# Second feed-forward matrix in seven block products

## The chip, the cores and the metric

One core of one Trainium2 chip runs the whole program. The metric is the device time of one execution in microseconds (us). The kernel before takes 877.99 us, the median of three runs (877.97 to 878.5).

## The reference

One decoder layer over 512 tokens of 1024 channels, float32. A combined projection feeds three token mixers (sparse attention, a gated recurrence, a short convolution), whose gated sum is projected and added to `x`. The part that changes is the last line:

```python
h = _rmsnorm(x, ln_mlp_g[l])
x = x + jnp.square(jax.nn.relu(h @ w_mlp_up[l])) @ w_mlp_down[l]
```

`w_mlp_up` is 1024 x 4096, `w_mlp_down` 4096 x 1024. The norm divides by the root of the mean square `ms + eps`; since relu squared is homogeneous of degree 2, the kernel leaves the division out of the first product and divides the second by `ms + eps`.

## The kernel before

Activations lie channel by token: a tile is 128 channels by 512 tokens. Weights come in slabs of 128 x 1024 float32 (512 KB each, `slabs_of` and `_layout`), loaded by SP's queue into three `raw` tiles (`loader`). `splitter` makes two reduced-precision tiles of each: `whi`, a copy rounded by ScalarE (L296), and `wlo`, what is left, subtracted by VectorE (L300). Every product of float32 values is then three TensorE matmuls (L334) into one PSUM bank: high by high, high by low, low by high, each with a 128 x 128 stationary block and up to 512 moving columns.

The order of work is written once, when the kernel is built. `make_plan` lists the weight tiles; the main task issues their matmuls in that order, and all other work is a set of tasks that a planner (`Order`) places by costs and ready times into each engine's instruction order. Each engine then runs its list in order; between engines semaphores hold what isn't ready. `Get` takes a buffer from a numbered pool (tags such as `whi`, `wlo` with four tiles, `w2` with 55, `w4` with six), `Need` waits for a named result, `spawn` starts a task (priority 0 or 1), and work of priority 1 is not placed over 0.9 us ahead of TensorE's planned time (`LIM`).

In the feed-forward part the plan has two halves: 16 up tiles (128 inner channels each, eight contraction steps, 24 matmuls of 512 columns), then eight down tiles over those 16 inner tiles (48 matmuls of 512 columns, `tall`). `ev_up` takes an up tile out of PSUM: relu and square on ScalarE, square again and the low part on VectorE. `ev_dn` multiplies a down tile by the reciprocal of the mean square (`R2`); in the first half GpSimd adds it to the residual tile `X1`, in the second VectorE adds and SP's queue stores the result.

Of the kernel before, what the change touches and what calls it, by code (L numbers as in the profile page):

```python
# [16 lines left out]
ALU = mybir.AluOpType  # L17
# [30 lines left out]
def slabs_of(name, j):  # L48

    if name in FIRST_COL:  # L50
        return [("in", 0, 8, FIRST_COL[name] + 128 * j, 128)]
    if name == "kv":
        return [("kv", 0, 3, 0, 324), ("kv", 384, 3, 0, 324), ("kv", 768, 2, 0, 324)]
    if name in ("hi", "aq"):
        return [("in", 256 * i, 2, C_HI if name == "hi" else C_AQ, 512) for i in range(4)]
    if name[0] == "u" and name != "up":
        return [(name, 0, 4, 512 * j + 256 * i, 256) for i in range(2)]
    if name in ("wo", "up"):
        return [(name, 0, 8, 128 * j, 128)]
    return [("dn", 2048 * (j // 8) + 1024 * i, 8, 128 * (j % 8), 128) for i in range(2)]  # L60


SLABS = [p for name, j in PLAN for p in slabs_of(name, j)]


class Op:
    __slots__ = ("e", "c", "ins", "outs", "f")

    def __init__(self, e, c, ins, outs, f):
        self.e, self.c, self.f = e, c, f  # L70
# [24 lines left out]
class Order:  # L95
# [41 lines left out]
    def run(self, op):  # L137
        start = max([self.clk[op.e], self.clk["PE"]] + [self.seen(k, op.e) for k in op.ins])
        end = start + op.c
        self.clk[op.e] = end  # L140
        if op.e == "D":
            end += 2000
# [107 lines left out]
def kernel(ctx: ExitStack, tc: tile.TileContext, xT, x, first_d, slabs, vecs, rel, ident_d, masks_d,  # L250
# [9 lines left out]
    def maker(pool, tag, shape, n):  # L260
# [4 lines left out]

    tags = {t: maker(pool, t, s, n) for t, pool, s, n in (
        ("raw", sp, (128, 1024), 3), ("whi", sp, (128, 1024), 4), ("wlo", sp, (128, 1024), 4),
        ("w2", sp, (128, 512), 55), ("w4", sp, (128, 1024), 6), ("am", sp, (128, 512), 2),
        ("p", sp, (128, 1280), 2), ("cmb", sp, (128, 1280), 1), ("st", sp, (128, 16), 8),
        ("toep", sp, (128, 2048), 1), ("acc", pp, (128, 512), 4), ("aux", pp, (128, 512), 4))}  # L270
    o = Order(tags)
# [56 lines left out]
    def mm(ps, a, b, start, stop):  # L328
        n = size(b)
        if a.dtype == F32R:  # L330
            c = 0.4167 * n + 13.5 if n >= 192 else 213
        else:
            c = 2 * max(0.84 * n, 55 if size(a) <= 64 else 0.65 * size(a)) + 4
        return Op("PE", c, [a, b] + ([] if start else [ps]), [ps], lambda: PE.matmul(ps, a, b, start=start, stop=stop))  # L334

    def tr(ps, a):
        k = a.shape[0]
# [56 lines left out]
    def loader():  # L394
        for k in range(8):
            r = yield Get("w4", "raw0")
            yield dma(r[:, :896], first_d[:, 896 * k:896 * (k + 1)], nbytes=896 * 512)
            put(("raw0", k), r)
        for n in range(NSL):
            r = yield Get("raw", "raw")  # L400
            w = SLABS[n][2] * SLABS[n][4]
            yield dma(r[:, :w], slabs[n][:, :w], nbytes=1 << 19)
            put(("raw", n), r)
            if n < 2:
                for tb in ((0, 1), (2, 3))[n]:
                    for i in range(2):
                        t = yield Get("w2", "xt")
                        yield dma(t, x[:, tb, 512 * i:512 * (i + 1)], nbytes=1 << 18)
                        put(("xt", tb, i), t)
            if n == 1:  # L410
                yield dma(ident, ident_d, nbytes=1 << 16)
                yield dma(caus, caus_d, nbytes=1 << 16)
            if n == 4:
                yield dma(masks.rearrange("p a b -> p (a b)"), masks_d, nbytes=1 << 18)

    def first():
        for k in range(8):
# [15 lines left out]
            put(("xl", k), xl[k])  # L433
            free(r)

    def splitter():
        for n in range(NSL):
            r = yield Need(("raw", n))
# [315 lines left out]
    def soft_task():  # L754
# [5 lines left out]
        for h in range(8):  # L760
# [14 lines left out]
            for tb in range(4):  # L775
# [9 lines left out]
        for t in mbs[1:]:  # L785
            free(t)

    def soft_block(h, tb, pl, pb, cb, st, p):
        n = pb.shape[1]
# [199 lines left out]
    def ev_wo(m, ps):  # L989
# [17 lines left out]
        if m == 7:  # L1007
            pm = yield Get("aux", "pm")
            yield mm(pm, ones, ssum[0], True, True)
            free(ssum[0])  # L1010
            yield ts(R2, pm, EPS, None, ALU.add)
            free(pm)
            yield recip(R2, R2)
            put("R2", True)

    def ev_up(m, ps):
        rl = yield Get("w2", "rl")
        yield act(rl, ps, AF.Relu)
        free(ps)
        hi_t = yield Get("w2", "hh", F32R)  # L1020
        yield act(hi_t, rl, AF.Square)
        yield tt(rl, rl, rl, ALU.mult)
        lo_t = yield Get("w2", "hl", F32R)
        yield tt(lo_t, rl, hi_t.bitcast(F32), ALU.subtract)
        free(rl)
        put(("h", m), (hi_t, lo_t))

    def ev_dn(f, m, ps):
        yield Need("R2")
        if f == 0:  # L1030
            t = yield Get("w2", "t")
            yield tt(t, ps, R2, ALU.mult)
            free(ps)
            yield tt(X1[m], X1[m], t, ALU.add, "G")
            free(t)
            put(("x1", m), True)
            return
        yield Need(("x1", m))
        t = yield Get("w2", "o")
        parts = 2 if m == 7 else 1  # L1040
        w = 512 // parts
        for i in range(parts):
            q = slice(w * i, w * (i + 1))
            yield tt(t[:, q], ps[:, q], R2[:, q], ALU.mult)
            yield tt(t[:, q], t[:, q], X1[m][:, q], ALU.add)
            yield o.ready[key(t)]
            yield dma(out[128 * m:128 * (m + 1), q], t[:, q], [t], nbytes=(1 << 18) // parts)
        free(ps, t)


    def cols(n, m0, name, ev, rhs):
# [87 lines left out]
            spawn(ev_iq(i, ps[i]), 0)  # L1139
        spawn(EV["hf"](0, ps[2]), 0)  # L1140

    def tall(n, f, m):
        ps = yield Get("acc", "Adn")
        for i in range(2):
            h, l, h3, l3 = yield Need(("w", n + i))
            for k in range(8):
                bh, bl = yield Need(("h", 16 * f + 8 * i + k))
                yield [mm(ps, h3[:, k], bh, i + k == 0, False), mm(ps, h3[:, k], bl, False, False),
                       mm(ps, l3[:, k], bh, False, i == 1 and k == 7)]
            free(h, l)  # L1150
        spawn(ev_dn(f, m, ps), 0)
# [4 lines left out]
    def main():  # L1156
        yield from start()
        n = 0
        for name, j in PLAN:
# [24 lines left out]
            elif name == "kv":  # L1184
                yield from rows(n, cnt, name, ev_kv, xc, 324)
            elif name in ("aq", "hi"):
                yield from rows(n, cnt, name, ev_rows(name), ncl, 512)
            elif name == "wo":
                yield from cols(n, j, name, ev_wo, mr)
                if j == 7:  # L1190
                    for k in range(8):
                        free(*S["mx", k])
            else:
                yield from tall(n, j // 8, j % 8)
                if j % 8 == 7:
                    for k in range(16):
                        free(*S["h", 16 * (j // 8) + k])
            n += cnt

    o.ready[key(vec)] = 1500.0  # L1200
# [39 lines left out]

def _layout(inp):
    w = {"in": inp["w_in"][0], "u0": inp["w_up_attn"][0], "u1": inp["w_up_hgrn"][0], "u2": inp["w_up_conv"][0],
         "wo": inp["w_out"][0], "up": inp["w_mlp_up"][0], "dn": inp["w_mlp_down"][0]}
# [40 lines left out]
```

## Time and profile before

| | |
|---|---|
| median of three runs | 877.99 us |
| profiled execution | 877.3 us |
| its span, first to last instruction | 875.5 us |
| matmuls and weight loads on TensorE | 4140 each |
| VectorE, ScalarE, GpSimd instructions | 953, 593, 67 |
| HBM read, written | 87.15 MB, 3.68 MB |

PE is TensorE, PEld its loads of the stationary block, DVE VectorE, ACT ScalarE, POOL GpSimd, SP the queue that issues most DMAs. A matmul's duration in a row runs from its start to the end of its results, so that neighbours overlap; the spacing of starts is what a matmul costs in a stream. In a group of instructions "out<-in" names tiles, and "idle before" is the time in which the engine stood before them, with what ended it. A wait row names who waited for whom.

### The profile page before, as it was taken

The numbers are of one execution on the slowest core, as the hardware profiler recorded it, in microseconds if no ns is written. First come the engines' busy times: TensorE is split into PE (matmuls) and PEld (weight loads), VectorE is DVE, ScalarE is ACT, GpSimd is POOL, SyncE is SP. The second block draws the span as 40 slices with busy tenths as digits, with TensorE's granted clock in tenths as the row PEclk, the third lists the DMA queues.
The fourth block names the chain that finished last, engine by engine and source line by source line (L and its number), as shares of the span: only waits on it lengthen the run. The fifth ranks groups of instructions, "written<-read, shape, count | busy, mean of one in ns | idle before, by whom it ended". The sixth has DMA issues, their size and how long they took to land.

```text
span 875.5 us, 10712 instructions
## 1 busy us (share of the span) xinstructions
PE 870.0 (99%) x4140; PEld 725.8 (83%) x4140; DVE 522.9 (60%) x953; ACT 357.6 (41%) x593; POOL 67.8 (8%) x67
## 2 busy tenths in 40 slices
PE   9999999999999999999999999999999999999997
PEld 7988888888888888888888888888888888888886
DVE  5679888888877785668438545444433344443331
ACT  7773435235443465656533443333111133331110
POOL 0001000020000211225000230000111100000000
PEclk9999999999999999999999999999999999999999
DMA  9553222222222212222224322222223222223310
GB/s 347 210 197 143 96 89 80 73 86 83 72 73 73 95 51 73 72 73 74 96 73 157 133 99 92 97 97 97 96 97 97 97 96 97 97 97 124 122 67 24
DMA packets 28587, 89.95 MB, mean 103 GB/s; under 512 B 3152, under 2 KB 5880, under 8 KB 28536
## 3 DMA queue, kind: packets, MB, share of 16 engines
q1 hardware_dynamic: 28392, 89.25, 29.6%
q8 instruction: 32, 0.52, 0.2%
q14 instruction: 19, 0.16, 0.1%
q10 hardware_dynamic: 144, 0.02, 0.0%
HBM read 87.15 MB, written 3.68 MB: 104 GB/s over the span
## 4 chain that ended last, share of the span: by engine, by line
PE 99%; DVE 0%; issue 0%
PE Aup L334 20%; PE Adn L334 20%; PE Ag L334 15%; PE Au L334 8%; PE Awo L334 5%; PE Acb L334 3%; PE Ahg L334 3%; PE Ach L334 3%; PE Aaq L334 3%; PE Acc L334 3%; PE Ahq L334 2%; PE Ahi L334 2%; PE pa L334 2%; PE Ahf L334 2%; PE Akv L334 2%; PE Ast L334 2%
## 5 line engine op out<-in xcount | busy, mean ns | idle before, releaser
L300 DVE TENSOR_TENSOR wlo<-raw,whi 128x1024 fp32r<-128x1024 f32 (+2 forms) x150 | 188.6, 1258 | 91.9 <-ACT whi L296 86.5
L296 ACT ACTIVATE whi<-raw 128x1024 fp32r<-128x1024 f32 (+2 forms) x150 | 153.9, 1026 | 217.8 <-PE Adn L334 120.1
L334 PE MATMUL Aup<-x2h,whi 128*128 128x512 f32 x256 | 100.0, 391 | 0.0
L334 PE MATMUL Aup<-x2h,wlo 128*128 128x512 f32 x256 | 99.6, 389 | 0.0
L334 PE MATMUL Aup<-x2l,whi 128*128 128x512 f32 x256 | 99.6, 389 | 0.0
L334 PE MATMUL Adn<-hh,whi 128*128 128x512 f32 x256 | 99.6, 389 | 0.0
L334 PE MATMUL Adn<-hl,whi 128*128 128x512 f32 x256 | 99.6, 389 | 0.0
L334 PE MATMUL Adn<-hh,wlo 128*128 128x512 f32 x256 | 99.6, 389 | 0.0
L334 PE MATMUL Ag<-nh,whi 128*128 128x512 f32 x192 | 78.1, 407 | 0.0
L300 DVE TENSOR_TENSOR rl<-rl 128x512 f32<-128x512 f32 x32 | 22.1, 692 | 91.4 <-ACT hh L296 91.4
L334 PE MATMUL Ag<-nh,wlo 128*128 128x512 f32 x192 | 75.2, 392 | 0.0
L334 PE MATMUL Ag<-nl,whi 128*128 128x512 f32 x192 | 75.0, 390 | 0.0
L296 ACT ACTIVATE rl<-Aup 128x512 f32<-128x512 f32 x32 | 19.1, 598 | 110.2 <-PE Aup L334 110.2
L334 PE MATMUL Au<-yp,whi 128*128 128x512 f32 x192 | 60.9, 398 | 0.0
L334 PEld LDWEIGHTS Aup<-x2l,whi 128*128 128x128 f32 x256 | 48.0, 188 | 10.3 <-issue 0.2
L334 PEld LDWEIGHTS Aup<-x2h,whi 128*128 128x128 f32 x256 | 48.0, 188 | 10.2 <-issue 0.2
L334 PEld LDWEIGHTS Adn<-hh,whi 128*128 128x128 f32 x256 | 48.0, 188 | 10.0
L334 PEld LDWEIGHTS Adn<-hl,whi 128*128 128x128 f32 x256 | 48.0, 188 | 10.0
L334 PEld LDWEIGHTS Aup<-x2h,wlo 128*128 128x128 f32 x256 | 48.1, 188 | 9.9
L334 PEld LDWEIGHTS Adn<-hh,wlo 128*128 128x128 f32 x256 | 48.0, 188 | 9.9
L334 PEld LDWEIGHTS Ag<-nh,wlo 128*128 128x128 f32 x192 | 36.0, 188 | 8.1
L334 PEld LDWEIGHTS Ag<-nh,whi 128*128 128x128 f32 x192 | 36.1, 188 | 6.2
(257 smaller groups left out, 1609.1 us busy)
## 6 DMA issues: line engine op xcount, KB each, us to landing
raw<-in_slabs_dram SPq DMA_DIRECT2D x139, 512.0 KB, 3.2
raw<-in_first_dram SPq DMA_DIRECT2D x8, 448.0 KB, 5.4
xt<-in_x_dram SPq DMA_DIRECT2D x8, 256.0 KB, 6.6
xr<-in_xT_dram SPq DMA_DIRECT2D x8, 256.0 KB, 4.0
x<-in_xT_dram SPq DMA_DIRECT2D x4, 512.0 KB, 5.9
out_dram<-o SPq DMA_DIRECT2D x7, 256.0 KB, 2.0
d<-d SPq DMA_DIRECT2D x1, 1536.0 KB
toep<-d SPq DMA_DIRECT2D x1, 1024.0 KB, 6.6
```

What stands on the lines that cost most here:

```text
L296: return Op("A", c, [in_, scale, bias], [out_, accum], lambda: A.activation(out_, in_, func, **kw))
L300: return Op(e, c, [a, b], [out_], lambda: (V if e == "V" else G).tensor_tensor(out_, a, b, op))
L334: return Op("PE", c, [a, b] + ([] if start else [ps]), [ps], lambda: PE.matmul(ps, a, b, start=start, stop=stop))
```

## The change

The second matrix is multiplied by 2 x 2 x 2 blocks with seven products in place of eight (Winograd's variant of Strassen's form). The 4096 inner channels are taken in four parts; each part holds four pairs of up tiles, and its down products follow when the part is ready: the plan has 9, 8, 8 and 7 up tiles ahead of the four parts. A unit is one part and one pair of output tiles, so there are 16. In it A is 2 x 2: output tile by half of the pair, 128 x 512 of weights each; B is 2 x 2: half of the pair by half of the tokens, 256 columns each.

- Weights (`seven`, `halves`): S1 = a21 + a22 is made by a plain load of a22 and an accumulating DMA of a21 from GpSimd's queue; S2 = S1 - a11, S3 = a11 - a21, S4 = a12 - S2 on VectorE; then a11|a12 and S2|S3 (1024 columns), S1, S4 and a22 (512) are split in high and low parts. The low part of a22 is made by a second accumulating DMA onto the negated high part.
- Activations (`ev_up`, `pair_of`): of each pair T1 = b12 - b11, T2 = b22 - T1, T3 = b22 - b12, T4 = b21 - T2 on VectorE, all split in high and low parts.
- Products (`twin_units`): two units take turns, step by step, one in the `acc` and one in the `aux` banks. Step 0 is a11 b11, step 1 a12 b21, then S2 T2, S3 T3, S1 T1, a22 T4, S4 b22. Step 2 and later ones add onto a bank that an earlier step left; before that the bank's content has been added to `X1`, and the step waits for it (`wait`).
- `ev_dn` adds each step's bank (256 columns) to `X1` on VectorE: seven for a unit. `X1` is multiplied by the mean square ahead of it, on GpSimd, and by the reciprocal at the end, on VectorE.
- The planner's cost of a matmul under 320 columns is 3 ns less; `Op` has a latency `lat`; `w2` has one tile more.

```diff
-    for f in range(2):
-        plan += [("up", 16 * f + j) for j in range(16)] + [("dn", 8 * f + j) for j in range(8)]
+    ups = [("up", j) for j in range(32)]
+    for c, (i, j) in enumerate(((0, 9), (9, 17), (17, 25), (25, 32))):
+        plan += ups[i:j] + [("dn", 4 * c + m) for m in range(4)]
...
+    def add_dma(out_, in_, ins):
+        return Op("G", 900, ins + [out_], [out_], lambda: G.dma_start(out_, in_, accum_op=ALU.add), 4600)
...
+            if n in UNITS:
+                g = yield Get("w4", "s1")
+                yield dma(g[:, :512], slabs[n + 1][:, 512:], nbytes=1 << 18)
+                yield add_dma(g[:, :512], slabs[n + 1][:, :512], [])
+                put(("s1", n), g)
...
+    def halves(src, w, name, big=True, dma_=False):
+        h = yield Get("whi" if big else "w2", "whi", F32R)
+        yield act(h[:, :w], src, AF.Copy)
+        l = yield Get("wlo" if big else "w2", "wlo", F32R)
+        if dma_:
+            yield act(l[:, :w], src, AF.Copy, scale=-1.0)
+            yield add_dma(l[:, :w], src, [src])
+            put(name, (h, l))
+            return
+        yield tt(l[:, :w], src, h[:, :w].bitcast(F32), ALU.subtract)
+        put(name, (h, l))
+
+    def seven(n):
+        r0 = yield Need(("raw", n))
+        r1 = yield Need(("raw", n + 1))
+        a11, a12, a21, a22 = r0[:, :512], r0[:, 512:], r1[:, :512], r1[:, 512:]
+        spawn(halves(r0, 1024, ("s", n, 0)), 1)
+        g = yield Need(("s1", n))
+        s = yield Get("toep", "sums")
+        s2, s3, s1, s4 = s[:, :512], s[:, 512:1024], g[:, :512], g[:, 512:]
+        yield tt(s2, s1, a11, ALU.subtract)
+        yield tt(s3, a11, a21, ALU.subtract)
+        spawn(halves(s[:, :1024], 1024, ("s", n, 1)), 1)
+        yield tt(s4, a12, s2, ALU.subtract)
+        spawn(halves(s1, 512, ("s", n, 2), False), 1)
+        spawn(halves(a22, 512, ("s", n, 3), False, True), 1)
+        spawn(halves(s4, 512, ("s", n, 4), False), 1)
...
+    def ev_dn(key_, m, q, ps, done, last):
+        yield Need(("x1", m))
+        yield tt(X1[m][:, q], ps[:, :256], X1[m][:, q], ALU.add)
+        put(key_, True)
+        if done:
+            free(ps)
+        if last:
+            t = yield Get("w2", "o")
+            yield tt(t[:, :256], X1[m][:, q], R2[:, q], ALU.mult)
+            yield o.ready[key(t)]
+            yield dma(out[128 * m:128 * (m + 1), q], t[:, :256], [t], nbytes=1 << 17)
             free(t)
...
+        steps = ((0, 0, "b11", 0, True, 0, LATE, False), (0, 1, "b21", 1, True, 0, LATE, True),
+                 (1, 0, "t2", 0, False, 1, LATE, False), (1, 1, "t3", 2, True, 1, EARLY, False),
+                 (2, 0, "t1", 0, False, 1, EARLY, True), (3, 0, "t4", 2, False, 1, LATE, True),
+                 (4, 0, "b22", 0, False, 0, EARLY, True))
+        wait = {2: 0, 4: 2, 5: 3, 6: 4}
...
+            for p in ps_:
+                bh, bl = yield Need(("hp", 4 * c + p, b))
+                w = slice(512 * half_ + 128 * p, 512 * half_ + 128 * (p + 1))
+                yield [mm(d, h[:, w], bh, new and p == 0, False, sk), mm(d, h[:, w], bl, False, False, sk),
+                       mm(d, l[:, w], bh, False, p == 3, sk)]
...
+        for ps_ in ((0, 1, 2), (3,)):
+            for i in (0, 1):
+                for u in (0, 1):
+                    yield from product(u, i, ps_)
+        for i in range(2, 7):
+            for u in (0, 1):
+                yield from product(u, i, (0, 1, 2, 3))
```

## Rows read from the trace of the kernel before

**Rows 1.** page, part 1: busy us (share of the span) xinstructions.
```profile
PE 870.0 (99%) x4140; PEld 725.8 (83%) x4140; DVE 522.9 (60%) x953; ACT 357.6 (41%) x593; POOL 67.8 (8%) x67
```

**Rows 2.** chain that ended last, from 520 us: start us, us, what.
```profile
609.85 87.04 PE Adn L334 x384
783.93 87.05 PE Adn L334 x384
871.00 0.44 DVE o L300
```

**Rows 3.** windows, the four feed-forward stages: columns in its first line.
```profile
core 0: us, PE busy (x) PEld busy (x) DVE busy (x) ACT busy (x) POOL busy (x), PEclk, DMA share, GB/s
609.60:696.80 87.20, 87.20 (x387) 72.19 (x386) 32.97 (x25) 18.09 (x19) 9.06 (x7) 1.00 0.31 102
sum 349.20, PE 349.20 PEld 288.51 DVE 141.70 ACT 97.95 POOL 12.14; mean PE 87.30 PEld 72.13 DVE 35.43 ACT 24.49 POOL 3.04
```

**Rows 4.** waits, feed-forward part: us in total, times, longest.
```profile
ACT whi L296 <- PE Adn L334: 120.1, 28, 4.4
```

**Rows 5.** waits of SP's queue, feed-forward part, same columns.
```profile
SPq L342 <- DVE wlo L300: 274.4, 58, 13.8
```

**Rows 6.** timeline, TensorE, 411.4 us: start us, us, engine, line, operation.
```profile
411.47 0.28 PE L334 MATMUL po<-ph,vst 128*128 128x256 f32 x1
...
412.19 0.34 PE L334 MATMUL pl<-kh,qs 128*128 128x384 f32 x1
```

**Rows 7.** timeline, TensorE near 290 us.
```profile
290.11 0.28 PE L334 MATMUL pl<-kh,qs 128*128 128x256 f32 x1
...
290.58 0.43 PE L334 MATMUL pa<-Am 128*120 128x64 f32 x3
```

**Rows 8.** timeline, TensorE near 24 us.
```profile
24.00 0.31 PE L334 MATMUL Akv<-whi,xhi 128*128 128x324 f32 x1
...
24.89 0.31 PE L334 MATMUL Akv<-whi,xhi 128*128 128x324 f32 x1
```

**Rows 9.** timeline, VectorE near 523 us.
```profile
522.88 1.23 DVE L300 TENSOR_TENSOR wlo<-raw,whi 128x1024 fp32r<-128x1024 f32 x1 [0.23 <-ACT whi L296]
```

**Rows 10.** groups by shape, VectorE, feed-forward part: busy us, mean ns, idle.
```profile
L300 DVE TENSOR_TENSOR hl<-rl,hh 128x512 fp32r<-128x512 f32 x32 | 21.8, 685 | 0.0
...
L300 DVE TENSOR_TENSOR o<-Adn,R 128x256 f32<-128x256 f32 x2 | 0.8, 420 | 9.5 <-PE Adn L334 9.5
```

**Rows 11.** groups by shape, VectorE, whole span, 256 columns.
```profile
L300 DVE TENSOR_TENSOR pl<-pt,ph 128x256 fp32r<-128x256 f32 x8 | 3.3, 416 | 3.6 <-ACT ph L296 3.6
```

**Rows 12.** groups by shape, ScalarE, feed-forward part.
```profile
L296 ACT ACTIVATE whi<-raw 128x1024 fp32r<-128x1024 f32 x61 | 64.5, 1057 | 123.4 <-PE Adn L334 120.1 <-issue 3.2
L296 ACT ACTIVATE hh<-rl 128x512 fp32r<-128x512 f32 x32 | 19.8, 622 | 0.0
```

**Rows 13.** timeline, all engines, the end of the span.
```profile
870.58 0.39 PE L334 MATMUL Adn<-hh,wlo 128*128 128x512 f32 x1
871.00 0.42 DVE L300 TENSOR_TENSOR o<-Adn,R 128x256 f32<-128x256 f32 x1 [9.46 <-PE Adn L334]
...
872.26 0.43 DVE L300 TENSOR_TENSOR o<-o,x 128x256 f32<-128x256 f32 x1
```

**Rows 14.** timeline, GpSimd and VectorE near 632.5 us.
```profile
632.42 1.29 POOL L300 TENSOR_TENSOR x<-x,t 128x512 f32<-128x512 f32 x1 [9.59 <-DVE t L300]
...
632.57 2.23 DVE L300 TENSOR_TENSOR wlo<-raw,whi 128x1024 fp32r<-128x1024 f32 x1 [0.23 <-ACT whi L296]
```

**Rows 15.** tile xr, eight loads of 256 KB: time to landing.
```profile
DMA to landing us min/median/max: 2.9/4.0/8.1
```

**Rows 16.** groups by shape, weight loads.
```profile
L334 PEld LDWEIGHTS Adn<-hh,whi 128*128 128x128 f32 x256 | 48.0, 188 | 10.0
```

**Rows 17.** timeline, weight loads near 411.5 us.
```profile
411.48 0.19 PEld L334 LDWEIGHTS po<-pl,vst 128*128 128x128 f32 x1
411.59 0.19 PEld L334 LDWEIGHTS pl<-kh,qs 128*128 128x128 f32 x1
```

More of the change, by code (lines that the diff above doesn't have):

```diff
@@ L59, in slabs_of, with __init__ @@
         return [(name, 0, 8, 128 * j, 128)]
-    return [("dn", 2048 * (j // 8) + 1024 * i, 8, 128 * (j % 8), 128) for i in range(2)]
+    return [("dn", 1024 * (j // 4), 8, 256 * (j % 4) + 128 * i, 128) for i in range(2)]
 SLABS = [p for name, j in PLAN for p in slabs_of(name, j)]
+UNITS = [n for n, p in enumerate(SLABS) if p[0] == "dn"][::2]
 class Op:
-    __slots__ = ("e", "c", "ins", "outs", "f")
-    def __init__(self, e, c, ins, outs, f):
-        self.e, self.c, self.f = e, c, f
+    __slots__ = ("e", "c", "ins", "outs", "f", "lat")
+    def __init__(self, e, c, ins, outs, f, lat=0):
+        self.e, self.c, self.f, self.lat = e, c, f, lat
         self.ins = [key(a) for a in ins if not isinstance(a, (int, float, type(None)))]
@@ L140, in run @@
         self.clk[op.e] = end
-        if op.e == "D":
-            end += 2000
+        end += 2000 if op.e == "D" else op.lat
         for k in op.outs:
@@ L326, in mset, with mm @@
         return Op(e, 60 + 0.6 * size(out_), [], [out_], lambda: (V if e == "V" else G).memset(out_, v))
-    def mm(ps, a, b, start, stop):
+    def mm(ps, a, b, start, stop, more=False):
         n = size(b)
         if a.dtype == F32R:
-            c = 0.4167 * n + 13.5 if n >= 192 else 213
+            c = 0.4167 * n + (10.5 if n < 320 else 13.5) if n >= 192 else 213
         else:
             c = 2 * max(0.84 * n, 55 if size(a) <= 64 else 0.65 * size(a)) + 4
-        return Op("PE", c, [a, b] + ([] if start else [ps]), [ps], lambda: PE.matmul(ps, a, b, start=start, stop=stop))
+        return Op("PE", c, [a, b] + ([] if start else [ps]), [ps], lambda: PE.matmul(ps, a, b, start=start, stop=stop, skip_group_check=more))
     def tr(ps, a):
@@ L434, in first @@
             free(r)
+    def halves(src, w, name, big=True, dma_=False):
[24 more added lines that the diff above has]
+        spawn(halves(s4, 512, ("s", n, 4), False), 1)
+        yield Need(("s", n, 0))
+        free(r0)
+        yield Need(("s", n, 1))
+        free(s)
+        yield Need(("s", n, 3))
+        free(r1)
+        yield Need(("s", n, 2))
+        yield Need(("s", n, 4))
+        free(g)
     def splitter():
         for n in range(NSL):
+            if SLABS[n][0] == "dn":
+                if n in UNITS:
+                    if n > UNITS[0]:
+                        yield Need(("s", UNITS[UNITS.index(n) - 1], 1))
+                    if UNITS.index(n) % 4 == 2:
+                        for p in range(UNITS.index(n) - 2, UNITS.index(n) + 2):
+                            for k in ("b11", "b21", "t2", "t4"):
+                                yield Need(("hp", p, k))
+                    spawn(seven(n), 1)
+                continue
             r = yield Need(("raw", n))
@@ L784, in soft_task @@
                     free(q)
-        for t in mbs[1:]:
-            free(t)
+            if h % 4 == 3:
+                free(kh, kl)
+        free(toep, *mbs[1:])
     def soft_block(h, tb, pl, pb, cb, st, p):
@@ L1010, in ev_wo @@
             free(ssum[0])
-            yield ts(R2, pm, EPS, None, ALU.add)
+            yield ts(R, pm, EPS, None, ALU.add)
             free(pm)
-            yield recip(R2, R2)
+            yield recip(R2, R)
             put("R2", True)
+            for j in range(8):
+                yield tt(X1[j], X1[j], R, ALU.mult, "G")
+                put(("x1", j), True)
     def ev_up(m, ps):
-        rl = yield Get("w2", "rl")
-        yield act(rl, ps, AF.Relu)
-        free(ps)
-        hi_t = yield Get("w2", "hh", F32R)
@@ L1021, in ev_up @@
[L1021 to L1032, printed above, removed]
-            free(ps)
-            yield tt(X1[m], X1[m], t, ALU.add, "G")
-            free(t)
[L1036 to L1048, printed above, removed]
+        p = m // 2
@@ new lines, in ev_up @@
+        if m % 2 == 0:
+            t = yield Get("p", "h")
+            put(("h0", "t", p), t)
+            yield act(t[:, :512], ps, AF.Relu)
+            free(ps)
+            yield act(t[:, :512], t[:, :512], AF.Square)
+            yield tt(t[:, 1024:], t[:, :256], t[:, 256:512], ALU.subtract)
+            put(("h0", "r", p), True)
+            return
+        t = yield Need(("h0", "t", p))
+        yield act(t[:, 512:1024], ps, AF.Relu)
+        free(ps)
+        yield act(t[:, 512:1024], t[:, 512:1024], AF.Square)
@@ new lines, in ev_up @@
+        yield Need(("h0", "r", p))
+        b12, b11, b22, b21, t1 = (t[:, 256 * i:256 * (i + 1)] for i in range(5))
+        u = yield Get("am", "hu")
+        t2, t3, t4 = u[:, :256], u[:, 256:], b12
+        spawn(pair_of(p, t[:, 256:768], ("b11", "b22")), 0)
+        spawn(pair_of(p, t[:, 768:1280], ("b21", "t1")), 0)
+        yield tt(t2, b22, t1, ALU.subtract)
+        yield tt(t3, b22, b12, ALU.subtract)
+        spawn(pair_of(p, u, ("t2", "t3")), 0)
+        yield tt(t4, b21, t2, ALU.subtract)
@@ new lines, in ev_up, with pair_of @@
+        x = yield Get("w2", "hx", F32R)
+        yield act(x[:, :256], t4, AF.Copy)
+        yield tt(x[:, 256:], t4, x[:, :256].bitcast(F32), ALU.subtract)
+        put(("hp", p, "t4"), (x[:, :256], x[:, 256:]))
+        hops[p].append(x)
+        for k in ("b11", "b21", "t2"):
+            yield Need(("hp", p, k))
+        free(t, u)
+    hops = [[] for _ in range(16)]
+    def pair_of(p, src, names):
+        h = yield Get("w2", "hh", F32R)
+        yield act(h, src, AF.Copy)
+        l = yield Get("w2", "hl", F32R)
+        yield tt(l, src, h.bitcast(F32), ALU.subtract)
+        hops[p].extend((h, l))
+        for i, k in enumerate(names):
+            put(("hp", p, k), (h[:, 256 * i:256 * (i + 1)], l[:, 256 * i:256 * (i + 1)]))
@@ L1140, in start, with twin_units, product @@
         spawn(EV["hf"](0, ps[2]), 0)
[L1142 to L1151, printed above, removed]
+    def twin_units(n, c, m):
+        steps = ((0, 0, "b11", 0, True, 0, LATE, False), (0, 1, "b21", 1, True, 0, LATE, True),
[3 more added lines that the diff above has]
+        wait = {2: 0, 4: 2, 5: 3, 6: 4}
+        regs = [[], []]
+        def product(u, i, ps_):
+            a, half_, b, r, new, mo, q, end = steps[i]
+            nn = n + 2 * u
+            h, l = yield Need(("s", nn, a))
+            if len(regs[u]) <= r:
+                regs[u].append((yield Get(("acc", "aux")[u], "Adn")))
+            d = regs[u][r][:, :256]
+            if i in wait:
+                yield Need(("e", nn, wait[i]))
+            sk = not new
+            for p in ps_:
[3 more added lines that the diff above has]
+                       mm(d, l[:, w], bh, False, p == 3, sk)]
+            if 3 in ps_:
+                spawn(ev_dn(("e", nn, i), 2 * (m + u) + mo, q, regs[u][r], i in (1, 5, 6), end and c == 3), 0)
+                if i in (1, 3, 4, 5, 6):
+                    free(h, l)
+        for ps_ in ((0, 1, 2), (3,)):
[5 more added lines that the diff above has]
+                yield from product(u, i, (0, 1, 2, 3))
     EV = dict(hf=ev_cols("z"), hq=ev_hq, hg=ev_hg, cc=ev_cc, ch=ev_ch, cb=ev_cb, up=ev_up,
@@ L1193, in main @@
             else:
[L1194 to L1197, printed above, removed]
+                if j % 2 == 0:
+                    yield from twin_units(n, j // 4, j % 4)
+                if j % 4 == 3:
+                    for p in range(4):
+                        free(*hops[j - 3 + p])
             n += cnt
```

5 lines of the change are left out of this document (3 added, 2 removed).

## The prediction

> **What bounds the kernel now.** I read the busy times first. TensorE is busy 870.0 of 875.5 us, VectorE 522.9, ScalarE 357.6, GpSimd 67.8 [rows 1]; the reader is to see that only one engine is full. The chain that ended last says the same in order of time: in the down products it is TensorE alone, and each stretch of 384 of them takes 87.04 or 87.05 us, that is 226.7 ns a matmul of 512 columns; VectorE comes into it only behind the last one [rows 2]. The windows by stage then show the room beside it. In the four stages of the feed-forward part (one stands as a row) the granted clock is 1.00, the 2.4 GHz level; VectorE is busy 141.7 of 349.2 us, ScalarE 97.95, and the DMA share of the second stage is 0.31 [rows 3]. ScalarE waits 120.1 us for down products to free a split buffer, and SP's queue 274.4 us for the splits to free a raw tile: supply runs ahead of TensorE, and is held back by buffers alone [rows 4, 5]. So time comes off only with TensorE's matmuls, as long as the other engines keep up.
>
> **TensorE's share.** Before, the second matrix takes 768 matmuls of 512 columns: 174.1 us [rows 2]. After, there are 16 units (four parts of the inner channels by four pairs of output tiles), each of seven products of 4 x 3 matmuls of 256 columns: 16 x 84 = 1344. What does one cost? The trace has them only in short runs, between 512s. Six in a row begin at 411.47 us and the next form at 412.19: 120 ns each; a run of four at 290.11 to 290.58 gives 117.5 [rows 6, 7]. A long run of 324 columns has 148 ns (24.00 to 24.89, six steps) [rows 8], of which 135 are columns at 2.4 GHz; the fixed part of 13 agrees with the 512's (226.7 less 213.3) and gives 120 for 256. I take 119, between the two runs: 159.9 us, with ends of 157.9 and 161.3. The saving is 14.2 us (12.8 to 16.2). So 1/8 fewer columns (21.8 us) lose a third to the fixed part, which is now paid 1344 times.
>
> The Trainium skill, "TensorE: Matmul & The Clock Gate", section "Back-to-back issue gap", gives N/2.4 + 2.5 ns for an isolated stream; by it the two sums would be 165.7 and 146.8, a saving of 19.0. The trace differs (226.7 where the page has 215.8), and it decides.
>
> The up products stay as they are: 768 in 349.2 - 174.1 = 175.1 us [rows 2, 3], 5.45 a tile of 24.
>
> **VectorE's share.** Prices: subtracting 1024 columns 1.23 us, 512 columns 0.685, 256 columns 0.42 out of PSUM and 0.416 out of SBUF [rows 9 to 11]. A unit now has two subtractions of 1024 (the low parts of a11|a12 and of S2|S3) and five of 512 (S2, S3, S4, two low parts): 5.9 us, where two slabs cost 2.5. A pair of up tiles has five of 256 and three of 512: 4.2, where it had 4 x 0.69 = 2.8. Evictions are 7 x 16 of 256: 47, and 16 closing multiplications in the last part: 7. With 32 up splits (39) and some 5 of statistics the sum is 94 + 67 + 47 + 7 + 39 + 5 = 259 us of the 335 that TensorE will need (175 + 160): 77%, against 41% before. ScalarE: a unit 2 x 1.057 + 4 x 0.62 = 4.6, a pair 7 x 0.62 + 0.4 = 4.7, 32 splits 34: about 183 of 335 [rows 12]. Both fit on average, so I count them at nothing but for the waits below; if that cover is gone, every microsecond over goes to the end.
>
> It is close in one place. Buffers of 1024 columns hold two units, so units 3 and 4 of a part are split while 1 and 2 run (a "twin", 2 x 84 x 119 ns = 20.0 us): 14 evictions 6.0 + 2 x 5.9 = 17.8, or 89%. Units 1 and 2 are split beside the up products: 8 x 5.45 = 43.6 us of TensorE against at most 10 + 17 + 12 = 39 of VectorE, less what was split earlier.
>
> **The new wait.** Step 2 adds onto the bank of step 0, so TensorE must wait until VectorE has read step 0. An eviction starts 0.42 us after the start of a last 512 matmul of 0.39 [rows 13]; with 0.28 for 256 columns [rows 6] that is 0.32, plus 0.42 of work and some 0.1 back: 0.84. Between the last matmul of step 0 and the first of step 2 lie ten matmul slots: 1.19. The margin is 0.35 for the first unit of a twin, and 1.8 for the second, which has step 2 of the first ahead of it. Behind the waiting matmul stands all of TensorE. If VectorE is in a 1.23 us subtraction, up to 0.9 is lost. The other three waits have 36 matmuls, 4.3 us, of cover. Eight twins at 0 to 0.9, or 2.8 with two subtractions ahead in both units: I take 0.5, so 4 (0 to 22). The last part has no extra up tile before it: its first products need 0.42 + 4 x 0.62 + 0.69 = 3.6 us (relu, square, two copies, one subtraction) from the last up tile, against 36 matmuls, 4.3 us, that don't need that tile. I take 0.5 (0 to 2).
>
> **The end, GpSimd and the queues.** Before, VectorE's four 256-column operations end 2.11 us after the start of the last matmul [rows 13]. After, one eviction and one multiplication do: 0.32 + 0.42 + 0.05 + 0.42 = 1.2, a gain of 0.9 (0 to 0.9). GpSimd loses eight additions of 1.29 us in the middle of the down products and gets eight multiplications by the mean square among the first up products; either takes about 1 us from a VectorE subtraction beside it (2.23 for 1.23) [rows 9, 14], covered in both places. SP's queue gets a further 256 KB load a unit, whose buffer comes free long before; at a DMA share of 0.31 this is nothing (0 to 2). The one operation that no row shows is the accumulating DMA from GpSimd, two a unit. The changed planner holds 0.9 us of GpSimd and 4.6 to landing. The nearest row is a plain 256 KB load, 2.9 to 8.1 us, median 4.0 [rows 15]. I take the planner's order as met: cost 0 (0 to 12, below).
>
> The Trainium skill, "DMA: Bandwidth & Descriptors", section "Anatomy of one DMA — SWDGE (gpsimd) path", fits such a DMA as 2.0 us + bytes/436e3; an estimate from that page is 2.6 us for 256 KB, by which no sum would wait. No run here shows it yet.
>
> **Sum.** The profiled execution took 877.3 (span 875.5 and 1.8 around it): 877.3 - 14.2 - 0.9 + 4 + 0.5 = 866.7. The median of the runs is 0.7 above the profiled one: 867.4.
>
> **Rivals.**
> 1. VectorE's order eats most of the gain. Splits are emitted up to 0.9 us ahead of TensorE's planned clock, so an eviction can find one or two before it. For: 89% in a twin. Against: of the eight waits of a twin seven have 1.8 us or more of cover. At 1.3 us a twin the loss is 10.4 instead of 4: 873.8. The range of this case is 873 to 876.
> 2. The slower side: the sums stand on a late accumulating DMA. S2 needs S1 = a21 + a22, which that DMA makes, and VectorE's queue is in order: while S2 waits, evictions wait behind it, and TensorE behind them. With a landing L the wait is S = L - 5.5 a unit. A first twin of a part has 2.2 us to spare for two units, so four of them lose 4 x (2S - 2.2). This decides from S = 2.5, L = 8: gain gone. At the slowest plain landing, 8.1, it is 12 us: 879.4; at 10 it is 27: 895. Against: median 4.0.
> 3. Loads of the stationary operand set the pace. Each load is recorded with 188 ns [rows 16], more than 119. If they could not overlap, 1344 x 188 ns = 252.7, 78.6 us more than before: about 956. Against: in the run of 256 columns loads of 0.19 us start 0.11 us apart, each overlapping the next [rows 17]. The Trainium skill, the page on TensorE, section "What overlaps and what doesn't", lets a load overlap running matmuls only on other row groups, which would bring this about; the trace does not agree, since loads of 0.19 us lie beside matmuls 0.12 us apart.
>
> **Chances.** Forecast 0.62, on its own 861 to 873; rival 1 0.13; a result between, within 0.2% of before (876.2 to 879.7; less than that a measurement of this kernel can't tell from no change) 0.06; rival 2 beyond that 0.17; rival 3 0.02. Faster is 0.75, same 0.06, slower 0.19. The low end takes the cheaper matmul and no waits: 877.3 + 0.7 - 16.2 - 0.9 = 860.9, and 2 more for what the planner may move elsewhere: 859. The high end lies between rival 2 at the slowest plain landing (879.4) and two subtractions ahead of every step 2 (866.7 - 4 + 22 + 0.7 = 885.4): 884. Outside is rival 3 and the later landings of rival 2.
>
> **What would show it.** 1344 down matmuls 117.5 to 120 ns apart within a step; idle TensorE only before step 2, under a microsecond each, and after the last up tile; VectorE at about 75 to 80% from 520 us on; the accumulating DMA landing within 5.5 us, S2 not waiting for it; evictions about 0.32 us behind a last matmul's start. I am wrong if the matmul spacing is 125 ns or more, if TensorE stands over 2 us a twin, or if the part before 520 us moves by over 2 us because the planner orders it anew.

## The result, and the profile after

The changed kernel takes 867.81 us (median of 4 runs, 867.41 to 869.2), the kernel before on the same chip 878.15 (877.97 to 878.5): a ratio of 0.9885 [0.9867, 0.9902]. The forecast was 867.4. The profiled execution took 867.56 with a span of 865.7, against 877.3 and 875.5 before.

Part 1 of the page, busy us and share of the span, answers to [rows 1]:

```profile
PE 858.9 (99%) x4716; PEld 743.4 (86%) x4716; DVE 614.4 (71%) x1199; ACT 422.2 (49%) x721; POOL 100.0 (12%) x99
```

TensorE is still the only full engine. VectorE has gained 91.5 us of work; what this cost TensorE is 3.06 us of stands, worked out below. Where the time went is in the chain of waits (start us, us, what), which answers to [rows 2]:

```profile
572.39 40.31 PE Adn L335 x336
...
656.25 40.31 PE Adn L335 x336
...
740.11 40.31 PE Adn L335 x336
...
823.15 11.88 PE Adn L335 x95
...
836.15 7.90 DMA raw<-in_slabs_dram
...
846.70 0.33 DVE o L301
847.03 0.34 DVE x L301
847.36 0.33 DVE o L301
847.70 1.15 DVE wlo L301
...
848.89 12.99 PE Adn L335 x106
```

In three of the four parts the 336 down products follow one another with nothing in between: 40.31 us by 336 is 120.0 ns each. In the fourth other engines come into the chain twice: in front of 823.15, and between 835 and 848.89, where first a load of weights stands in it and then VectorE's own order of work, two closing multiplications (`o`) among it. The groups of waits (us in total, times, longest) from 515 us on name the releasers:

```profile
PEld Adn L335 <- DVE x L301: 0.4, 2, 0.3
PE Adn L335 <- DVE wlo L301: 1.8, 1, 1.8
DVE sums L301 <- DMA s<-in_slabs_dram: 0.3, 1, 0.3
```

The first is the wait of step 2 for an eviction (`x`), ahead of its weight load: it came twice. The second is TensorE's one long stand, for the split of S2 and S3 of the last unit. The third is all that VectorE waited for an accumulating DMA, in 16 units. The windows by stage (us; busy of each engine; granted clock, DMA share, GB/s), a middle part, the last part and the sum from 522.4 us on:

```profile
656.10:696.40 40.30, 40.30 (x337) 40.30 (x336) 29.07 (x52) 15.65 (x21) 2.61 (x3) 1.00 0.58 159
...
818.30:861.60 43.30, 41.25 (x338) 40.44 (x336) 31.95 (x66) 14.31 (x23) 4.06 (x5) 1.00 0.45 116
sum 339.20, PE 337.15 PEld 305.89 DVE 234.29 ACT 163.06 POOL 42.26; mean PE 42.14 PEld 38.24 DVE 29.29 ACT 20.38 POOL 5.28
```

The last part is 3.0 us longer than the others at the same clock of 1.00 (2.4 GHz), and VectorE does more in it. Inside a step, TensorE's timeline (start us, us, engine, line, operation):

```profile
660.16 0.28 PE L335 MATMUL Adn<-hl,whi 128*128 128x256 f32 x1
...
660.64 0.28 PE L335 MATMUL Adn<-hh,wlo 128*128 128x256 f32 x1
...
662.20 0.28 PE L335 MATMUL Adn<-hh,whi 128*128 128x256 f32 x1
```

From 660.16 to 662.20 lie 17 steps: 120 ns each, where [rows 6, 7] had 120 and 117.5 in short runs. The matmul at 660.64 is the last of step 0. VectorE's timeline shows what follows it:

```profile
660.96 0.42 DVE L301 TENSOR_TENSOR x<-Adn,x 128x256 f32<-128x256 f32 x1 [1.01 <-PE Adn L335]
661.30 0.42 DVE L301 TENSOR_TENSOR h<-h 128x256 f32<-128x256 f32 x1
661.63 0.42 DVE L301 TENSOR_TENSOR x<-Adn,x 128x256 f32<-128x256 f32 x1
```

The eviction starts 0.32 us behind that matmul's start. Two things more stand here: VectorE was idle for 1.01 us ahead of it, and operations recorded with 0.42 us start 0.33 apart when one follows another.

The decomposition of the span, 875.5 to 865.7: the down matmuls 174.1 to 1344 x 0.120 = 161.3 (-12.8); TensorE's stands between them +3.06, all of them in the last part: in its first twin 0.46 for the low part of the last up tiles and 0.22 ahead of step 2, in its last twin 0.32 ahead of step 2 and 2.06 for the split; the end, from the last matmul's start to the span's end, 4.94 to 4.12 (-0.8); the first up product begins 0.62 later (522.38 against 521.76), a lag that is there at the first product behind the warm-up matmuls already (6.18 against 5.51) and that differs from execution to execution (5.5 to 6.7 in the profiles of these runs), so the change is not its cause. Together -9.9, against -9.8.

### The profile page after: what moved, and what is told of

Its sections match the earlier page's. It is cut to its first block, busy times and chain, and to the rows that moved or that the text cites. A ratio compares the mean times of both kernels' runs of the same rounds, so it can differ in the third digit from the quotient of the medians.

```text
span 865.7 us, 12437 instructions
## 1 busy us (share of the span) xinstructions
PE 858.9 (99%) x4716; PEld 743.4 (86%) x4716; DVE 614.4 (71%) x1199; ACT 422.2 (49%) x721; POOL 100.0 (12%) x99
## 4 chain that ended last, share of the span: by engine, by line
PE 97%; DVE 1%; DMA 1%; issue 0%; ACT 0%; SPq 0%; DVEq 0%
PE Aup L335 20%; PE Adn L335 17%; PE Ag L335 15%; PE Au L335 8%; PE Awo L335 5%; PE Acb L335 3%; PE Ahg L335 3%; PE Ach L335 3%; PE Aaq L335 3%; PE Acc L335 3%; PE Ahq L335 3%; PE Ahi L335 3%; PE pa L335 2%; PE Ahf L335 2%; PE Akv L335 2%; PE Ast L335 2%
## 5 line engine op out<-in xcount | busy, mean ns | idle before, releaser
L301 DVE TENSOR_TENSOR wlo<-raw,whi 128x1024 fp32r<-128x1024 f32 (+2 forms) x134 | 162.4, 1213 | 95.7 <-ACT whi L297 95.5
L297 ACT ACTIVATE whi<-raw 128x1024 fp32r<-128x1024 f32 (+3 forms) x150 | 146.3, 978 | 143.8 <-issue 30.9
L335 PE MATMUL Adn<-hh,wlo 128*128 128x256 f32 x384 | 108.8, 283 | 1.8 <-DVE wlo L301 1.8
L335 PE MATMUL Adn<-hl,whi 128*128 128x256 f32 x384 | 108.7, 283 | 0.2 <-DVE hl L301 0.2
L335 PE MATMUL Adn<-hh,whi 128*128 128x256 f32 x384 | 108.9, 283 | 0.1
L301 DVE TENSOR_TENSOR x<-Adn,x 128x256 f32<-128x256 f32 x112 | 46.2, 422 | 41.4 <-PE Adn L335 41.3
L335 PEld LDWEIGHTS Adn<-hh,wlo 128*128 128x128 f32 x384 | 73.7, 192 | 2.0 <-DVE wlo L301 2.0
L335 PEld LDWEIGHTS Adn<-hh,whi 128*128 128x128 f32 x384 | 73.7, 192 | 0.6 <-DVE x L301 0.4
L335 PEld LDWEIGHTS Adn<-hl,whi 128*128 128x128 f32 x384 | 73.7, 192 | 0.6 <-DVE hl L301 0.4
L297 ACT ACTIVATE h<-Aup 128x512 f32<-128x512 f32 x32 | 19.2, 598 | 88.6 <-PE Aup L335 88.6
```

The costliest lines, as they stand in the source:

```text
L297: return Op("A", c, [in_, scale, bias], [out_, accum], lambda: A.activation(out_, in_, func, **kw))
L301: return Op(e, c, [a, b], [out_], lambda: (V if e == "V" else G).tensor_tensor(out_, a, b, op))
```

## The experiments

Ratios are against the kernel before on the same chip. "Stands" are the sums of what lies beyond 120 ns between down matmuls. So they also hold what is lost while the granted clock is at 0.50, the 1.2 GHz level, where these matmuls start 213 ns apart in the traces.

**Both accumulating DMAs undone** (`e1_vec_sums`): S1 and the low part of a22 on VectorE.

```diff
-            if n in UNITS: ... add_dma(g[:, :512], slabs[n + 1][:, :512], [])
+        g = yield Get("w4", "s1")
...
+        yield tt(s1, a21, a22, ALU.add)
-        spawn(halves(a22, 512, ("s", n, 3), False, True), 1)
+        spawn(halves(a22, 512, ("s", n, 3), False), 1)
```

> The changed kernel with both accumulating DMAs undone: S1 = a21 + a22 and the low part of a22 are made by VectorE (two more operations of 512 columns a unit, 16 x 2 x 0.684 = 21.9 us of VectorE), and the extra 256 KB loads go. My theory: VectorE has room in the feed-forward part (its rows there add up to some 255 us of 339), but in a first twin of a part it was reckoned at 17.8 of 20 us, and 2.7 more would pass the 20; so TensorE would stand 0 to 1 us in each of four first twins: 868 to 872, against 867.8. Rival, that the DMAs are the danger and VectorE has ample room: the stand of 2.1 us before the last two units, which ends on a late load, goes, and the time is 865 to 867. Rival, that VectorE is nearly the bound: 878 or more.

Measured: 877.9 us, 0.9998 [0.9988, 1.0007]. The whole gain is gone: the rival of 878 was met to 0.1 us, my theory of 0 to 1 us a first twin was wrong. There are 13.7 us of stands, in the second twin of a part (3.9, 3.8, 2.3 and 0.8) and in the first of the last (2.9). The first twin of part 2 in the changed kernel (columns as above):

```profile
656.10:676.20 20.10, 20.10 (x169) 20.10 (x168) 16.81 (x31) 10.73 (x16) 1.74 (x2) 1.00 0.53 123
```

and the windows of part 2 with the accumulating DMAs undone:

```profile
659.80:679.90 20.10, 20.10 (x169) 20.10 (x168) 17.01 (x33) 7.90 (x12) 0.00 (x0) 1.00 0.30 95
...
687.20:689.60 2.40, 0.35 (x4) 0.15 (x3) 2.40 (x5) 0.29 (x1) 0.00 (x0) 1.00 0.67 213
689.60:691.60 2.00, 2.00 (x14) 2.00 (x15) 1.50 (x2) 0.00 (x0) 0.00 (x0) 0.83 0.07 29
691.60:694.60 3.00, 3.00 (x17) 3.00 (x17) 0.42 (x1) 1.06 (x1) 0.00 (x0) 0.54 0.48 178
```

and what comes before the stand and ends it, VectorE's timeline of the same kernel:

```profile
684.83 0.79 DVE L301 TENSOR_TENSOR x<-Adn,x 128x256 f32<-128x256 f32 x2 [1.08 <-PE Adn L335]
685.53 0.68 DVE L301 TENSOR_TENSOR wlo<-raw,whi 128x512 fp32r<-128x512 f32 x1
...
687.99 0.41 DVE L301 TENSOR_TENSOR x<-Adn,x 128x256 f32<-128x256 f32 x1
688.33 1.21 DVE L301 TENSOR_TENSOR wlo<-sums,whi 128x1024 fp32r<-128x1024 f32 x1
```

In the first twin VectorE is busy 17.01 of 20.10 us, that is 85%, and the changed kernel had 16.81 there without a stand: of the added work the twin took up 0.2 us. VectorE's queue is in order, and its idle 3.1 us are waits for a bank in front of evictions, where the planned order has no split. The splits that don't fit slip behind the next twin's start, and at 687.2 TensorE stands for one of them until 689.6. Even there a split that could run stands behind a wait: VectorE is idle for 1.08 us until the eviction at 684.83, and the low part at 685.53 comes behind it, though ScalarE had made its high part by 681.10. So what is full is this order of VectorE's work; whether another order would find room was not run. About 22 us more on VectorE (32 operations of 0.68) cost 10 us. In the profiled execution 3.1 of the 13.7 us are matmuls at the lower clock, behind the stands of parts 1 and 2 (for part 2 the clocks of 0.83 and 0.54 in the last two windows).

**A late accumulating DMA** (`e2_twice_added`): a second one behind the first, of which the planner knows nothing. It adds a21 twice, so this kernel no longer gives the layer's output.

```diff
...
                 yield add_dma(g[:, :512], slabs[n + 1][:, :512], [])
+                yield add_dma(g[:, :512], slabs[n + 1][:, :512], [], 0, 0)
```

> The changed kernel with a second accumulating DMA of a21 behind the first in every unit, of which the planner's costs know nothing (S1 becomes 2 a21 + a22, so the output is another). It lands some 5 us later than planned. The prediction's second rival, priced as there: landing 10.6 us, wait 5.1 us a unit, four first twins lose 2 x 5.1 - 2.2 = 8 each: 32 us, so 895 to 900. Against it: behind the accumulating DMA the planner places the load of a21 and a22 themselves, which S3 and S4 need anyway, and evictions have 4.3 us of cover in seven of eight waits; then a large part is covered and the time is 870 to 880. If nothing at all is lost, 867 to 869, the landing never mattered.

Measured: 897.45 us, 1.0218 [1.0201, 1.0235], in the range that rival 2's formula gave. The view of the tile `sums` has both ends of the wait (us, times):

```profile
  DMA s<-in_slabs_dram: 34.0, 9
...
  PE Adn L335: 8.6, 4
```

VectorE stood 34.0 us for the DMA. TensorE lost 34.0 us too, but not all of it by standing: the window of part 2's second twin has a mean granted clock of 0.88.

```profile
688.40:716.30 27.90, 23.64 (x170) 23.23 (x169) 16.76 (x29) 8.08 (x10) 0.86 (x1) 0.88 0.52 163
```

In the profiled execution the clock fell to 0.50 seven times between down products, and matmuls at that clock hold some 10 of the 34.0 us. The place is another than the formula had, too: it counted on the first twins, where part 1 lost 6.0 and part 4 4.2 but parts 2 and 3 nothing; the second twins lost 5.6, 7.7, 7.9 and 2.5. So the mechanism is shown, a late DMA that holds up VectorE and with it TensorE. That its 895 to 900 was met all the same is luck: of the 32 us that it gave, the waits alone make some 24.

**Narrow matmuls alone** (`e3_halved`): the kernel before, each down matmul of 512 columns as two of 256 in two banks.

```diff
...
+                for z in range(2):
+                    d, q = ps[z][:, :256], slice(256 * z, 256 * (z + 1))
+                    yield [mm(d, h3[:, k], bh[:, q], i + k == 0, False), mm(d, h3[:, k], bl[:, q], False, False),
+                           mm(d, l3[:, k], bh[:, q], False, i == 1 and k == 7)]
```

> The kernel before with each down matmul of 512 columns issued as two of 256 into two banks: eight products, no block sums, 1536 matmuls of 256 columns in place of 768 of 512. Theory, a fixed part of 13 ns a matmul: 1536 x 120 = 184.3 us against 174.1, so 10.2 us more than before: 888, and spacing 120 ns. If the fixed part of a matmul were 2.5 ns (the Trainium skill, TensorE: Matmul & The Clock Gate, Back-to-back issue gap), an estimate from that page is some 880. If weight loads of 188 ns set the pace: 1536 x 188 = 289, so 990.

Measured: 887.69 us, 1.0112 [1.0091, 1.0132]. The chain:

```profile
610.26 92.15 PE Adn L334 x768
```

92.15 by 768 is 120.0 ns, where one of 512 took 226.7 [rows 2]. So two halves cost 13.3 ns more than the whole, and this alone is 10 us over 768 pairs. Of 21.8 us that an eighth fewer columns is worth, the change loses 9.0 to the same fixed part.

**Units one after another** (`e4_one_by_one`): the two units of a twin no longer take turns.

```diff
-        for ps_ in ((0, 1, 2), (3,)): for i in (0, 1): for u in (0, 1): ...
+        for u in (0, 1): for ps_ in ((0, 1, 2), (3,)): for i in (0, 1): ...
```

> The changed kernel with the two units of a twin run one after the other, not in turns. Step 2 of a unit then follows the last matmul of step 0 by four matmul slots (0.48 us) and not by ten (1.19). An eviction was seen to start 0.32 us after that matmul's start, take 0.425, and release TensorE 0.055 later: 0.80. Theory: each of 16 units stands 0.32 us or a little more, 5 to 9 us, and the last part, whose first products then cover only 18 matmuls and not 36, loses up to 2 more: 873 to 879. Rival, that TensorE's queue or the planner hides the wait: 867 to 869.

Measured: 891.01 us, 1.0148 [1.0133, 1.0164]: a miss, the loss is over twice what I gave. Stands are 27.0 us; the waits:

```profile
PE Adn L335 <- DVE x L301: 15.4, 25, 1.7
```

In second twins, 1.0 us each, the two waits of step 2 are there with 0.48, where 0.32 was reckoned. First twins lose 5.7 each: I had left out that every later step's cover shrinks as well (36 matmuls or 4.3 us to 12 or 1.4), so that a split standing ahead of an eviction now costs. VectorE's timeline at one stand of 1.2 us, which ends at 670.20:

```profile
668.59 1.22 DVE L301 TENSOR_TENSOR wlo<-raw,whi 128x1024 fp32r<-128x1024 f32 x1
669.73 0.42 DVE L301 TENSOR_TENSOR x<-Adn,x 128x256 f32<-128x256 f32 x1
```

Taking turns is worth 23 us here, more than the seven products save.

**The changed kernel again** (`a1_changed`), on the chip of the next three:

> The changed kernel once more, beside the three below on the same chip: 867 to 869. Its stands in the last part (2.3 us before the last two units in the first profile, 0.7 behind the last up tile) should be there again, if they come from the order of work, and the first one should be of another length, if it comes from one load that happened to land late.

868.35 us (867.08 to 869.59), 0.989 [0.9875, 0.9906]. The stands are again 0.68 from 822.68 on, and 2.01 in the last twin, all of it for the split from 846.51 on: the 0.32 ahead of step 2 is gone. There VectorE had waited for the last slab, which lands at 843.62 here and at 844.05 in the first profile, with the eviction behind it in the queue. So this small part came from the load, the 2.0 us did not change with it.

**No extra up tile** (`e5_no_extra_up`): 8 up tiles ahead of each part.

```diff
-    for c, (i, j) in enumerate(((0, 9), (9, 17), (17, 25), (25, 32))):
+    for c, (i, j) in enumerate(((0, 8), (8, 16), (16, 24), (24, 32))):
```

> The changed kernel with 8 up tiles ahead of every part in place of 9, 8, 8, 7, so that the first three parts start right behind the last up tile that they need, as the fourth does. Theory: what the last pair needs (3.6 us and VectorE's other work) is longer than the 36 matmuls that don't need it; the fourth part stood 0.7 us there, so three more parts lose as much, 2 us: 869 to 872. Rival, that the supply of units 1 and 2 also leaned on that tile's time: 873 or more. Rival, that the tile was not needed: 867 to 868.

Measured: 870.77 us, 0.9918 [0.9903, 0.9932], as expected: a stand of 0.68 to 0.69 now opens each of the four parts. That is the price of a last up tile right ahead of its part, its low part (0.46) and the step 2 that follows (0.22) together. The last twin lost 3.57 in place of 2.38 (2.01 in the run before this one), and only some 2.0 of it are a stand; the windows of this kernel:

```profile
848.70:851.00 2.30, 0.52 (x5) 0.32 (x4) 2.30 (x5) 0.48 (x1) 0.00 (x0) 1.00 0.92 214
851.00:852.00 1.00, 1.00 (x9) 1.00 (x10) 0.99 (x2) 0.00 (x0) 0.00 (x0) 1.00 0.10 33
852.00:853.00 1.00, 1.00 (x8) 1.00 (x7) 0.42 (x1) 0.00 (x0) 0.00 (x0) 0.59 0.00 0
853.00:854.00 1.00, 1.00 (x6) 1.00 (x6) 0.00 (x0) 0.00 (x0) 0.00 (x0) 0.50 0.00 0
```

and of the changed kernel, behind the same stand:

```profile
846.80:849.00 2.20, 0.41 (x4) 0.20 (x3) 2.20 (x5) 0.42 (x1) 0.00 (x0) 1.00 0.94 216
...
851.00:852.00 1.00, 1.00 (x11) 1.00 (x10) 0.17 (x1) 0.00 (x0) 0.00 (x0) 1.00 0.00 0
```

TensorE stands as long in both, then the granted clock falls to 0.50 (1.2 GHz) in the one execution and stays at 1.00 in the other.

**What makes the stand of the last twin?** The chain above goes back through a slab that landed at 844.05. `e7_tile_only` gives the second slab of the third unit a free tile, so that it is loaded before:

```diff
-            r = yield Get("raw", "raw")
+            r = yield Get("cmb" if n - 1 in UNITS[2::4] else "raw", "raw")
...
```

> The changed kernel with one raw tile more: the second slab of the third unit of each part is loaded into the tile of the attention part that is long free (cmb). The last unit's slabs can then be loaded some 8 us earlier, and S3 of that unit does not wait for the load. Theory, that the stand before the last two units ends on the late load: 2 us go, 865 to 866.5. Rival, that VectorE's full order sets that stand: 867 to 868.5.

Measured: 869.69 us, 0.9905 [0.989, 0.992]: a miss. The last slab was issued at 833.0, and no wait for it is left, yet the stand is 1.91 us as before. VectorE's timeline of this kernel:

```profile
844.37 0.68 DVE L301 TENSOR_TENSOR sums<-raw,raw 128x512 f32<-128x512 f32 x1
846.24 0.79 DVE L301 TENSOR_TENSOR x<-Adn,x 128x256 f32<-128x256 f32 x2 [1.18 <-PE Adn L335]
846.94 0.68 DVE L301 TENSOR_TENSOR s<-raw,sums 128x512 f32<-128x512 f32 x1
847.54 0.75 DVE L301 TENSOR_TENSOR x<-Adn,x 128x256 f32<-128x256 f32 x2
848.20 0.41 DVE L301 TENSOR_TENSOR o<-x,R 128x256 f32<-128x256 f32 x1
848.76 0.42 DVE L301 TENSOR_TENSOR x<-Adn,x 128x256 f32<-128x256 f32 x1
849.10 0.41 DVE L301 TENSOR_TENSOR o<-x,R 128x256 f32<-128x256 f32 x1
849.43 1.22 DVE L301 TENSOR_TENSOR wlo<-sums,whi 128x1024 fp32r<-128x1024 f32 x1
```

The sums are ready at 845.05; the split that TensorE waits for stands at 849.43, behind S4, five evictions and two closing multiplications (`o<-x,R`), placed in this order. So the late load was not the cause of this stand. Other stands came up as well, 0.58 in the second twin of parts 1 to 3; why the planner puts these there I did not follow.

**Cover and tile together** (`e6_cover_and_tile`): as above, and in the last part's first twin the step S3 T3 is begun with the first two, so that more products come ahead of those on the last up tile.

```diff
...
+        first = (0, 1, 3) if c == 3 and m == 0 else (0, 1)
...
-            for i in (0, 1):
+            for i in first:
...
```

> The raw tile as in the one before, and in the first twin of the last part the first three parts of S3 T3 are done before anything that needs the last pair, so that 54 matmuls (6.5 us) and not 36 (4.3) cover its way through ScalarE and VectorE. Theory: 0.7 us less than with the tile alone: 864 to 866, the fastest of all. Rival, that the earlier S2|S3 split delays the pair's own work on VectorE: no gain against the tile alone, 865 to 867.5.

Measured: 869.62 us, 0.9903 [0.9886, 0.992]: a miss. The 0.68 behind the last up tile went, and 0.67 came ahead of an eviction at 833.1; the last twin's stand of 1.91 stayed, with the clock falling behind it (3.48 in all). The 0.58 of parts 1 to 3 are here as well.

**The closing multiplications later** (`e8_closing_later`): the order itself, if it is the cause.

```diff
         if last:
-            t = yield Get("w2", "o") ...
+            spawn(closing(m, q), 1)
+    def closing(m, q):
+        yield Need(("s", UNITS[-1], 1))
+        t = yield Get("w2", "o") ...
```

> The changed kernel with the closing multiplications (X1 by the reciprocal of the mean square, 16 of 256 columns) placed by a task of their own, behind the last S2|S3 split. With one raw tile more the stand before the last two units kept its 1.9 us, and VectorE's order there has two closing multiplications and four evictions ahead of that split: so the order of VectorE sets it, not the load. Theory: the stand goes or falls below 0.5 us, and with it the fall of the clock that followed it in some executions: 865.5 to 866.5, against 867.8 and 868.4, and the executions agree more closely. Rival, that units 15 and 16 are late through the whole chain of sums: 867.5 to 868.5.

Measured: 865.23 us (864.73 to 865.63), 0.9856 [0.984, 0.9873], faster than both kernels. The chain of this kernel:

```profile
823.15 36.36 PE Adn L335 x299
```

and VectorE's timeline:

```profile
844.06 0.42 DVE L301 TENSOR_TENSOR x<-Adn,x 128x256 f32<-128x256 f32 x1 [2.45 <-PE Adn L335]
844.40 1.22 DVE L301 TENSOR_TENSOR wlo<-sums,whi 128x1024 fp32r<-128x1024 f32 x1
845.54 0.75 DVE L301 TENSOR_TENSOR x<-Adn,x 128x256 f32<-128x256 f32 x2
```

From 823.15 to the last product TensorE now runs without a break; the split comes at 844.40 in place of 847.61, and the closing multiplications behind it. The last twin, which lost 2.38 us in the changed kernel, loses nothing. So the place of the closing multiplications is the cause, since the early load alone (`e7_tile_only`) left the stand as it was. The order shifts with them as a whole, not only by the two multiplications just ahead of the split (0.33 us each): the last slab is issued at 832.33 and not at 836.15, and the sums are ready at 841.0 and not at 844.8. What each of these is worth by itself was not run.

**Both** (`e9_later_and_cover`):

> As the one before, and in the first twin of the last part three parts of S3 T3 go ahead of what needs the last pair (54 matmuls of cover, not 36). With the raw tile this took away the 0.7 us stand behind the last up tile, and one of 0.7 came ten us later before an eviction, with VectorE full. Theory: with VectorE relieved of the closing multiplications the second does not come: 864.5 to 866. Rival, that the first twin is full of splits in any case: as the one before.

865.42 us, 0.986 [0.9845, 0.9874]: no better than without the cover. Stands fall from 0.69 to 0.34, but the profiled execution also began 0.48 later, so 0.35 us is below what the runs can tell.

## Why the prediction was right, step by step

- **TensorE's share**: right in kind, the term mis-sized. I took 119 ns, between two short runs of 120 and 117.5; it is 120.0, and the saving is 12.8 in place of 14.2, the low end of what I gave. The fixed part of 13 ns is shown by `e3_halved`. The sum by the Trainium skill, "TensorE: Matmul & The Clock Gate", section "Back-to-back issue gap", which has the gap of an isolated matmul, was a saving of 19.0; the trace doesn't agree (120.0 ns where N/2.4 + 2.5 gives 109). Weight loads (rival 3) cost nothing: they fill 40.30 of 40.30 us in the window of part 2, one every 120 ns, though each lasts 192 ns against 188 in [rows 16].
- **VectorE's sum** was too high as a busy time: 259 us of 335, measured 234.3 of 339.2, that is 69% where my sign asked for 75 to 80. I added durations, which do come to 258.5, but a row's 0.42 us is 0.33 where operations follow each other. What I made of the sum was more wrong than its size: I read 17.8 of 20.0 in a twin as 2.2 to spare. The twin had 16.8 and so more idle time than that, but `e1_vec_sums` shows that added work could use 0.2 us of it in this order.
- **The wait of step 2**: its working was exact (0.32 behind the last matmul, 0.42 of work), its price of 4 us was not met. In parts 1 to 3 the step starts about 0.5 us behind the eviction's end, without waiting, since the planner put no split just ahead of an eviction there; in the last part it waited in both twins, 0.54 us together, with a split or a sum just ahead of the eviction, much as I had described. That it is cover that keeps this wait small is shown by `e4_one_by_one`.
- **The last part** cost 3.06 and not 0.5: 0.46 for the last up tile, as I had it, the 0.54 of step 2, and 2.06 for a split, which I did not foresee. I counted the closing multiplications in VectorE's sum and did not ask what they stand ahead of (`e8_closing_later`). By my own sign, a stand of over 2 us in a twin, this step failed in one twin of eight.
- **The end**: 0.8 of 0.9. **The accumulating DMAs**: 0.3 us, and they issue for 0.90 and 0.94 us where I had 0.9; three of the 16 sums landed later than the 5.5 us of my sign, at most at 6.2, and S2 waited for one. Rival 2 didn't occur; `e2_twice_added` shows its mechanism, and its price only by luck.
- **The sum** was 866.7 for the profiled execution, measured 867.56. That it is as near as 0.9 us is in part luck: 1.4 us too much saving stands against 1.4 us too much waiting (4.5 for 3.06). Most of what is left is the 0.6 us by which this execution began its up products later.

## What to carry to other kernels

Fewer multiplications in narrower pieces are to be priced by the spacing of the narrow shape in a trace, and the work they move to an in-order engine by where in its queue it stands, not by its busy share: here a twin at 84% had no stand, and with more to do it came to 85% and no further. That is the limit of this order, not one of the engine that was shown. Accumulations that two independent units take in turns hide their evictions, worth 23 us here, and are to be checked first. Work that nobody waits for, such as a closing multiplication, is to be ordered behind the work that the bounding engine needs.

## What the runs showed of the hardware

The accumulating DMA of 256 KB, which no row before showed, lands much as a plain load does [rows 15]; the view of tile `s`, GpSimd's 16 issues alone, has

```profile
DMA to landing us min/median/max: 3.7/4.4/6.2
```

The estimate from the Trainium skill, "DMA: Bandwidth & Descriptors", section "Anatomy of one DMA — SWDGE (gpsimd) path", was 2.6. The trace does not agree: none of the 16 landed before 3.7.

After a stand of about 2 us TensorE's granted clock fell to 0.50 in some executions and not in others (the windows of `e5_no_extra_up` and of the changed kernel), for some 3 us and a loss of about 1.5 us beyond the stand. With both accumulating DMAs undone one execution has both: the clock fell behind the stands of 2.3 and 2.2 us in parts 1 and 2, and not behind that of 2.2 in part 3. The runs of the changed kernel lie at 867.1 to 868.1 and at 869.2 to 869.6, the upper ones with a mean granted clock of 0.997 to 0.998: this fits, but only the execution with a profile shows the place, so it stays open for the others. Such a stand thus cost up to 1.8 times its own length (3.57 us for some 2.0), a reason more to remove it.
